# Where the split token rows begin in on-chip memory, and the number of idle matmuls at the start

## The chip, the cores and the metric

The kernel runs as one program on one core of a Trainium2 chip. The metric is the device time of one execution in microseconds, taken as the median of several runs. The engines are TensorE (PE; the profile lists its weight loads apart, as PEld), VectorE (DVE), ScalarE (ACT), GpSimd (POOL) and SyncE (SP), which here only issues DMAs.

## The reference

One layer of a decoder trunk, for 4096 prompt tokens and 64 sample tokens (8 sequences of 8 tokens), width 1024:

```
h = rmsnorm(x) * g_pre
z = h @ w_in                       # 1024 -> 2816 columns, cut into ten groups
A) out_a = silu(cg) * cb * conv3(cc * ch)          # gated short convolution, 256 channels
B) out_b = silu(ag) * window_attention(q, k, v)    # window 128, 8 query heads, 2 kv heads, a sink per head
C) out_c = silu(mg) * memory_attention(mq)         # 4 heads into 256 memory tokens
y = concat(out_a, out_b, out_c) @ w_out            # 1024 -> 1024
x = x + rmsnorm(y) * g_post
```

The outputs are x for all tokens and the new keys, values and convolution rows. Everything is float32.

## The kernel before

**Two stages.** The first stage (`plain_block`, then `input_projection`) computes z for all 4160 tokens and writes the parts of it to DRAM. It takes the first 929 us of the profile. The second stage reads them back in chunks of 256 tokens, does both attentions and the output projection, and takes the rest.

**Split numbers.** TensorE multiplies in the reduced format float32r, so each operand is split in two: `hi` is the value rounded to that format, `lo` is what is left over. A product of two numbers is then three matmuls: hi·w_hi, lo·w_hi, hi·w_lo. `split` and `x_split` make the token halves: ACT writes `hi`, DVE writes `lo = x - hi`. `w_split` makes the weight halves in the same way.

**The first stage's matmuls.** Tokens are cut into 8 blocks of 520, each of two halves of 260 (`HW`). The width 1024 is cut into two halves of four 128-row pieces (`KH = 4`). Blocks 0 and 1 use plain products (8 per block), all others a scheme with 7 products per block (`PRODUCTS`), whose operands are sums and differences of token halves and of weight quarters. The columns of w_in go in three phases of 4, 4 and 3 pairs of 128-column tiles. One call of `product` is 12 matmuls, each with a weight tile of 128x128 (stationary) and 260 tokens (moving), added up in one PSUM bank `c`. There are 768 such matmuls in the plain blocks, 2016 in the rest of phase 0, 2688 in phase 1 and 2016 in phase 2, 7488 in all; every one loads its own weights. DVE adds the banks into the tiles `z` (`evict`).

**Order.** In the plain blocks and phase 0 the order of each engine is the order in which the code is written; later a scheduler sets it, with some instructions pinned.

**Where the operands lie.** An address here is that of a byte in each of the 128 partitions of on-chip memory, as the built program has it. A token half is a tile of four rows of 320 float32 (`XR = 320`), of which the first 260 are used. A row is thus 1280 bytes, 5 times 256, and all four rows of a tile begin at the same address modulo 256. The tiles come from the pool `hp` (two buffers for `hi`, two for `lo`). A weight tile is 2 x 512 float32 from the pools `wa` and `wb`; a matmul reads 128 of them, at a multiple of 512 bytes. The pool `shift` holds one tile of 32 float32 that nothing uses; it stands ahead of `hp` and moves it, and all pools opened after it on that side, by 128 bytes. In the program of before, the token rows and the weights both begin at 224 modulo 256.

Other matmuls of the program with float32r operands, in the same terms (moving operand, then weights, modulo 256):

| matmul | columns | moving | weights | count |
|---|---|---|---|---|
| `c`, first stage | 260 | 224 | 224 | 7488 |
| `y`, output projection (weights `mh`, `ml`) | 512 (256 in the last part) | 224 | 224 | 1560 |
| `y` of the sample tokens (weights `mh_s`) | 512 | 224 | 96 | 32 |
| `ws`, window scores | 256 | 96 or 160 | the same | 512 |
| `xs`, memory scores, odd chunks and the first | 256 | 160 | 160 | 144 |
| `xs`, memory scores, even chunks | 256 | 160 | 96 | 112 |

**The beginning.** While the first tokens and weights are on their way, TensorE runs 14 matmuls on a tile of ones (`idle<-warm`). Their result is not used.

Of the kernel before, what the change touches and what calls it, by code (L numbers as in the profile page):

```python
# [8 lines left out]
F32 = mybir.dt.float32  # L9
F32R = mybir.dt.float32r  # L10
# [5 lines left out]
P = 128  # L16
D = 1024
KT = D // P
KH = KT // 2
# [4 lines left out]
HW = 260  # L24
XR = 320
# [22 lines left out]
def f(ap):  # L48
    return ap.bitcast(F32)
# [3 lines left out]
def hybrid_layer(ctx: ExitStack, tc: tile.TileContext, a: dict):  # L53
# [31 lines left out]
    pa = ExitStack()  # L85
# [3 lines left out]

    place = ctx.enter_context(tc.tile_pool(name="place", bufs=1)).tile([P, 2, KH, HW], F32, name="place")  # L90
    hxp = pa.enter_context(tc.tile_pool(name="hx", bufs=4))
    pa.enter_context(tc.tile_pool(name="shift", bufs=1)).tile([P, 32], F32, name="shift")
    hp = pa.enter_context(tc.tile_pool(name="hp", bufs=2))
    own = ExitStack()
    kept_z = ExitStack()
# [66 lines left out]
    def store(dst, src):  # L162
        if store_queue[0] is G:
            G.dma_start(dst, src)
        else:
            late.append(lambda: DMA.dma_start(dst, src))
# [153 lines left out]
    def gain_of(o, k):  # L320
        kk = KH * (int(o[1]) - 1) + k
        return gpre[:, kk : kk + 1]
# [16 lines left out]
    def t_sum(ph, b, o):  # L339
# [9 lines left out]
        if ph == 1:  # L349
# [2 lines left out]
                tc.keep_in_program_order(ins)  # L352
            store(hd[b][o], ops[o])

    def split(src, name):
        hi = hp.tile([P, KH, XR], F32R, tag="hi", name=f"hi{name}")[:, :, :HW]
        lo = hp.tile([P, KH, XR], F32R, tag="lo", name=f"lo{name}")[:, :, :HW]
        S.copy(hi, src)
        V.tensor_tensor(lo, src, f(hi), op=ALU.subtract)
        return hi, lo  # L360
# [157 lines left out]
    def h_split(i):  # L518
        if i < len(steps):
            ph, b, p = steps[i]  # L520
            o = PRODUCTS[p][1]
            hs[i] = split(xs[ph, b][o], f"{ph}_{b}{o}")
# [52 lines left out]
    raw0, zz, pending, h0, kept = {}, {}, {}, {}, {}  # L575

    def x_split(b, o, meanwhile=lambda: None):
        x = xs[0, b][o]
        h0[b, o] = hi, lo = [hp.tile([P, KH, XR], F32R, tag=n, name=f"{n}0_{b}{o}")[:, :, :HW] for n in ("hi", "lo")]
        for k in range(KH):  # L580
            if k == 1:
                meanwhile()
            g = gain_of(o, k)
            S.mul(hi[:, k], x[:, k], g)
            V.scalar_tensor_tensor(lo[:, k], x[:, k], g, f(hi[:, k]), op0=ALU.mult, op1=ALU.subtract)
# [37 lines left out]
    def plain_jobs(b, s):  # L623

        gains = lambda b, *os: [lambda o=o: x_gain(0, b, o) for o in os]
        scales = lambda b, *os: [lambda o=o: x_scale(0, b, o) for o in os]
        parts = lambda b, o: [lambda: x_split(b, o)]
        fill = lambda o: [lambda q=q: first_fill(o, q) for q in range(4)]
        sums = lambda q, k: [lambda: first_sums(q, k)]
# [70 lines left out]
    idle = accumulator(1, 2, "idle")  # L700
    warm = hp.tile([P, KH, XR], F32R, tag="lo", name="warm").rearrange("p k n -> p (k n)")
    G.memset(f(warm[:, : P + 512]), 1.0)
    for n in (416, 416, 416, 416, 512, 512, 512, 416, 416, 416, 260, 260, 260, 260):
        TE.matmul(idle[:, 0, :n], warm[:, :P], warm[:, P : P + n], start=True, stop=True)  # L704
    x_split(0, "B11", lambda: first_fill("A21", 0))
    for q in range(4):
        if q > 0:
# [743 lines left out]
    class Block:  # L1451
# [10 lines left out]
        def split(self):  # L1462
# [13 lines left out]
            self.hl = [hi, lo]  # L1476

        def run(self, last, start, split, starts):
            b, m = self.b, self.m
            yn = work([P, D], "yn", f"yn{b}")  # L1480
# [4 lines left out]
            for p, (c0, c1) in enumerate(parts):  # L1485
                if p == 1:
                    split()
                acc = psum("z", f"y{b}_{p}")[:, : c1 - c0]
                j, passes = 0, 3 if m == P else 2
                for k in range(KT):  # L1490
                    if k in starts:
                        start()
                    for l, r in ((0, 0), (1, 0), (0, 1)) if m == P else ((0, 0), (0, 1)):
                        TE.matmul(acc, self.hl[l][:, k], wo[k][c0 // 512][:, r, c0 % 512 : c0 % 512 + c1 - c0], start=j == 0, stop=j == passes * KT - 1)  # L1494
                        j += 1
                if m < P:
                    S.copy(yn[:m, c0:c1], acc[m : 2 * m])
                    V.tensor_tensor(acc[:m], acc[:m], yn[:m, c0:c1], op=ALU.add)
                end = last and p == 2
                if not end:  # L1500
                    V.tensor_tensor(yn[:m, c0:c1], acc[:m], gpost[:m, c0:c1], op=ALU.mult)  # L1501
                S.activation((psum("t", "sq") if end else acc)[:m, : c1 - c0], acc[:m], AF.Square, scale=float(D) ** -0.5, accum_out=st[:m, p : p + 1])  # L1502
                if last and p == 1:
                    V.tensor_tensor(st[:m, 0:1], st[:m, 0:1], st[:m, 1:2], op=ALU.add)
# [180 lines left out]
```

## Time and profile before

| | |
|---|---|
| median of 3 runs | 1536.18 us (1535.31 to 1536.74) |
| profiled execution | 1533.46 us, of which the span of the core's instructions is 1531.7 us |
| granted TensorE clock in that execution | 0.999 |
| busy: PE, PEld, DVE, ACT, POOL | 1520.7, 1398.8, 1145.3, 806.1, 380.0 us |

A matmul's duration in the profile (283 ns for one with 260 columns) holds its way through the array, and successive matmuls overlap. What one costs in a long run is therefore read from starts: the start of the last minus the start of the first, over the number between them. The chain of work that ended last names, from the end back, what each step waited for; a piece "PE c L368 x1895" is a run of 1895 matmuls in which none waited for anything but the one before it. The profile prints names without the numbers of buffers, and `c`, `hi`, `lo` and `w` with those of block, quarter and product.

### The profile page before, as it was taken

What the parts mean: (1) busy time and instruction counts of PE and PEld (TensorE: products, weight loads), DVE (VectorE), ACT (ScalarE), POOL (GpSimd) and SP (SyncE); (2) the same over time, 40 slices, a digit from 0 to 9 for tenths busy, and PEclk for the clock granted to TensorE, in tenths of its full rate; (3) what the DMA queues carried; (4) which work ended last, traced back from release to release, by engine and by line L of the source; (5) the groups of instructions that cost most, each with busy time, mean ns of one, the idle gap of its engine ahead of it and who ended that gap; (6) DMA issues with size and microseconds to landing.
All of it is one profiled execution on the core that took longest, in us unless ns stands there. A gap on an engine that the chain in (4) does not pass through costs nothing.

```text
span 1531.7 us, 30162 instructions
## 1 busy us (share of the span) xinstructions
PE 1520.7 (99%) x11337; PEld 1398.8 (91%) x11337; DVE 1145.3 (75%) x2055; ACT 806.1 (53%) x2039; POOL 380.0 (25%) x604
## 2 busy tenths in 40 slices
PE   9999999999999999999999999999999999999998
PEld 9999999999999999999999998788888888888876
DVE  6789888898978777897777679766666666666743
ACT  6786566476222222354454447755665565565632
POOL 0223332221400000000101204544444444444310
PEclk9999999999999999999999999999999999999999
DMA  9989999878755333677877789977777777776332
GB/s 257 199 225 246 274 283 267 277 244 284 194 181 181 127 126 127 225 231 278 229 272 227 230 291 260 239 151 159 148 148 151 155 156 150 160 161 146 131 110 96
DMA packets 177942, 306.28 MB, mean 200 GB/s; under 512 B 33925, under 2 KB 107653, under 8 KB 177765
## 3 DMA queue, kind: packets, MB, share of 16 engines
q1 hardware_dynamic: 130901, 227.38, 48.2%
q0 software_dynamic: 46176, 75.92, 25.1%
q8 instruction: 90, 1.47, 0.4%
q10 hardware_dynamic: 720, 1.05, 0.2%
q14 instruction: 55, 0.45, 0.1%
HBM read 197.23 MB, written 108.05 MB: 199 GB/s over the span
## 4 chain that ended last, share of the span: by engine, by line
PE 93%; DVE 3%; DMA 1%; ACT 1%; issue 1%; POOL 0%; SPq 0%; DVEq 0%; POOLq 0%; ACTq 0%
PE c L368 53%; PE y L1494 23%; PE ws L1248 4%; PE wo L1090 2%; PE wt L1271 2%; PE xs L1184 2%; PE xt L1199 2%; PE wo L1220 2%; PE wo L1226 1%; PE mem_acc L791 1%; DMA nat<-in_x_p 1%; DMA ws18A<-in_w_in 0%; DMA ws20A<-in_w_in 0%; DVE x_2T L348 0%; PE idle L704 0%
## 5 line engine op out<-in xcount | busy, mean ns | idle before, releaser
L1494 PE MATMUL y<-wo,mh 128*128 128x512 f32 (+1 forms) x1040 | 350.1, 399 | 0.0
L375 DVE TENSOR_TENSOR z<-c,z 128x520 f32<-128x520 f32 (+1 forms) x308 | 195.0, 647 | 88.8 <-PE c L368 87.5
L1494 PEld LDWEIGHTS y<-wo,mh 128*128 128x128 f32 x1040 | 194.3, 188 | 39.3 <-issue 2.4
L1494 PE MATMUL y<-wo,ml 128*128 128x512 f32 (+1 forms) x520 | 201.8, 388 | 0.0
L1261 ACT ACTIVATE sm<-sm,wnm 128x128 f32<-128x128 f32 x256 | 99.6, 390 | 61.0 <-DVE wnm L1255 59.7
L1193 POOL TENSOR_SCALAR xp<-xp,xrd 128x256 f32<-128x256 f32 x128 | 74.6, 590 | 207.1 <-DVE xrd L1189 207.0
L1494 PEld LDWEIGHTS y<-wo,ml 128*128 128x128 f32 x520 | 98.2, 189 | 16.2
L1185 DVE TENSOR_REDUCE xmx<-xs 128x2 f32<-128x512 f32 x64 | 44.1, 689 | 59.4 <-PE xs L1184 59.3
L1273 ACT COPY wpt<-wt 128x512 f32<-128x512 f32 x64 | 37.3, 582 | 86.3 <-PE wt L1271 83.7
L1248 PEld LDWEIGHTS ws<-kst,q 128*128 128x128 f32 x512 | 70.0, 190 | 5.4 <-ACT xp L1188 0.7
L1501 DVE TENSOR_TENSOR yn<-y,gpost 128x512 f32<-128x512 f32 (+1 forms) x66 | 45.1, 684 | 39.6 <-PE y L1494 39.3
L1248 PE MATMUL ws<-kst,q 128*128 128x256 f32 x512 | 73.1, 283 | 0.4 <-ACT xp L1188 0.4
L1502 ACT ACTIVATE y<-y 128x512 f32<-128x512 f32 (+1 forms) x66 | 38.6, 585 | 64.2 <-DVE yn L1501 64.2
L739 POOL CAST wmask<-negs 128x256 uint8<-128x256 f32 x1 | 0.6, 610 | 266.4 <-DMA negs<-in_wmask 266.4
L1281 POOL TENSOR_SCALAR_AFFINE_SELECT wpt<-wpt 128x512 f32<-128x512 f32 x64 | 52.8, 824 | 42.1 <-ACT wpt L1273 39.1
L1188 ACT ACTIVATE xp<-xs,xnm 128x256 f32<-128x256 f32 x128 | 58.9, 464 | 7.1 <-DVE xnm L1186 7.1
L1123 POOL DMA_DIRECT2D q<-qd x64 | 42.8, 674 | 71.0 <-DVE wo L186 60.9
L1112 POOL DMA_DIRECT2D kst<-qd x64 | 38.6, 616 | 63.7 <-PE xt L1199 41.5
L1251 DVE COPY_PREDICATED sm<-wmask,ws 128x256 f32<-128x256 uint8 x124 | 52.2, 436 | 2.7 <-ACT sm L1250 2.5
L1512 DVE SCALAR_TENSOR_TENSOR xr<-yn,yst,xr 128x1024 f32<-128x1024 f32 (+2 forms) x34 | 43.1, 1269 | 14.0 <-POOL yst L1508 13.3
L1278 POOL TENSOR_SCALAR_AFFINE_SELECT wpv<-wpt 128x512 f32<-128x512 f32 x62 | 40.2, 648 | 50.9 <-ACT wpt L1273 50.8
L377 ACT COPY z<-c 128x520 f32<-128x520 f32 (+1 forms) x44 | 24.4, 554 | 51.9 <-PE c L368 47.9
(962 smaller groups left out, 5116.4 us busy)
## 6 DMA issues: line engine op xcount, KB each, us to landing
q<-qd POOLq DMA_DIRECT2D x64, 384.0 KB, 8.2
xr<-in_x_p SPq DMA_DIRECT2D x32, 512.0 KB
nat<-in_x_p SPq DMA_DIRECT2D x39, 416.0 KB
o_yp<-xr SPq DMA_DIRECT2D x31, 512.0 KB
md<-th POOLq DMA_DIRECT2D x48, 260.0 KB, 6.5
qd<-zh SPq DMA_DIRECT2D x48, 260.0 KB
qd<-z SPq DMA_DIRECT2D x48, 260.0 KB
kst<-qd POOLq DMA_DIRECT2D x60, 192.0 KB, 5.7
```

The costliest lines, as they stand in the source:

```text
L368: TE.matmul(bank[:, :HW], l, r, start=first and i == 0, stop=last and i == 3 * KH - 1)
L375: add = lambda dst, other: V.tensor_tensor(dst, c, other, op=ALU.add)
L1185: V.tensor_reduce(mx[:, :nb], s, axis=AX.X, op=ALU.max)
L1188: S.activation(p[:, i, :], s[:, i, :], AF.Exp, bias=nm[:, i : i + 1], scale=SCALE, accum_out=den[:, i : i + 1])
L1193: G.tensor_scalar(p[:, i, :], p[:, i, :], rd[:, i : i + 1], 0.5, op0=ALU.mult, op1=ALU.mult)
L1248: TE.matmul(s3[:, hh, :], self.q[:, 4 + 2 * (2 * half + hh) + kvh, i * P : i * P + P], self.kst[:, 2 * kvh + part, i * P : i * P + 2 * P], ...
L1251: V.copy_predicated(sm[:, 2 * half : 2 * half + 2, :], third["wmask"], third["negs"] if first else s3[:, :, 0:P])
L1261: S.activation(sm[:, hh, :], sm[:, hh, :], AF.Exp, bias=nm[:, hh : hh + 1], scale=SCALE, accum_out=den[:, hh : hh + 1])
L1281: G.affine_select(p3, p3, pattern=[[0, 4], [1, P]], compare_op=ALU.is_ge, fill=0.0, base=0, channel_multiplier=-1)
L1494: TE.matmul(acc, self.hl[l][:, k], wo[k][c0 // 512][:, r, c0 % 512 : c0 % 512 + c1 - c0], start=j == 0, stop=j == passes * KT - 1)
L1501: V.tensor_tensor(yn[:m, c0:c1], acc[:m], gpost[:m, c0:c1], op=ALU.mult)
L1512: V.scalar_tensor_tensor(self.xr[:m, cs], yn[:m, cs], st[:m, 3:4], self.xr[:m, cs], op0=ALU.mult, op1=ALU.add)
```

## The change

Three things change in the code:

- the pool `shift` is gone, so `hp` and the pools behind it on that side (`z0` to `z10`, `y0` to `y2`, `nat`, `ones` and the temporary tiles `t0`, `t1`, `t2a`, `t2b`) lie 128 bytes lower; `wa`, `wb`, `place`, `hx` and everything of the second stage lie where they lay;
- a token row begins 16 float32 (64 bytes) into its 320, in `split_tile`, for `hi` and for `lo`. With the 128 bytes less, the rows begin at 160 modulo 256, where they began at 224. The weights stay at 224;
- six of the fourteen idle matmuls are gone.

```diff
-    pa.enter_context(tc.tile_pool(name="shift", bufs=1)).tile([P, 32], F32, name="shift")
...
+    begins = {"hi": 16, "lo": 16}
+
+    def split_tile(tag, name):
+
+        n = begins[tag]
+        return hp.tile([P, KH, XR], F32R, tag=tag, name=name)[:, :, n : n + HW]
+
     def split(src, name):
-        hi = hp.tile([P, KH, XR], F32R, tag="hi", name=f"hi{name}")[:, :, :HW]
-        lo = hp.tile([P, KH, XR], F32R, tag="lo", name=f"lo{name}")[:, :, :HW]
+        hi, lo = split_tile("hi", f"hi{name}"), split_tile("lo", f"lo{name}")
...
-        h0[b, o] = hi, lo = [hp.tile([P, KH, XR], F32R, tag=n, name=f"{n}0_{b}{o}")[:, :, :HW] for n in ("hi", "lo")]
+        h0[b, o] = hi, lo = [split_tile(n, f"{n}0_{b}{o}") for n in ("hi", "lo")]
...
-    for n in (416, 416, 416, 416, 512, 512, 512, 416, 416, 416, 260, 260, 260, 260):
+    for n in (416, 416, 416, 416, 512, 512, 512, 416):
```

No instruction changes its place in the order of any engine. On TensorE, at the beginning of the program, these rows stood before (`idle` is the bank that nobody reads, `w_0A` the first quarter of the weights, `hi_0B` and `lo_0B` the first tokens):

```order
1 L704 MATMUL idle<-warm 128x416 x4
2 L704 MATMUL idle<-warm 128x512 x3
3 L704 MATMUL idle<-warm 128x416 x3
4 L704 MATMUL idle<-warm 128x260 x4
5 L368 MATMUL c_0_0_0_278<-hi_0B_240,w_0A_244 128x260
6 L368 MATMUL c_0_0_0_278<-lo_0B_241,w_0A_244 128x260
7 L368 MATMUL c_0_0_0_278<-hi_0B_240,w_0A_244 128x260 x2
```

And these stand there now:

```order
1 L709 MATMUL idle<-warm 128x416 x4
2 L709 MATMUL idle<-warm 128x512 x3
3 L709 MATMUL idle<-warm 128x416
4 L373 MATMUL c_0_0_0_268<-hi_0B_230,w_0A_234 128x260
5 L373 MATMUL c_0_0_0_268<-lo_0B_231,w_0A_234 128x260
6 L373 MATMUL c_0_0_0_268<-hi_0B_230,w_0A_234 128x260 x2
```

Two idle matmuls of 416 columns and four of 260 are missing; the first product follows the eighth. Lines of the kernel from 352 on have moved by five.

## The prediction

> **What bounds the kernel now.** I read the page first: busy time, the granted clock, the shares of the chain.
>
> ```profile
> span 1531.7 us, 30162 instructions
> ...
> PE 1520.7 (99%) x11337; PEld 1398.8 (91%) x11337; DVE 1145.3 (75%) x2055; ACT 806.1 (53%) x2039; POOL 380.0 (25%) x604
> ...
> PEclk9999999999999999999999999999999999999999
> ...
> PE 93%; DVE 3%; DMA 1%; ACT 1%; issue 1%; POOL 0%; SPq 0%; DVEq 0%; POOLq 0%; ACTq 0%
> PE c L368 53%; PE y L1494 23%; PE ws L1248 4%; PE wo L1090 2%; PE wt L1271 2%; PE xs L1184 2%; PE xt L1199 2%; PE wo L1220 2%; PE wo L1226 1%; PE mem_acc L791 1%; DMA nat<-in_x_p 1%; DMA ws18A<-in_w_in 0%; DMA ws20A<-in_w_in 0%; DVE x_2T L348 0%; PE idle L704 0%
> ```
>
> TensorE is busy nearly all the time at the full granted clock, and 93% of the chain is its work; the last row splits the chain by line. The second view is the chain in order of time, its pieces in the first stage; columns are start, duration, what, and how many.
>
> ```profile
> 6.53 50.52 PE c L368 x420
> ...
> 58.27 24.57 PE c L368 x208
> 82.84 9.36 DMA nat<-in_x_p
> ...
> 112.51 236.80 PE c L368 x1992
> ...
> 428.63 5.35 DMA ws18A<-in_w_in
> ...
> 479.46 225.15 PE c L368 x1895
> ...
> 876.57 52.04 PE c L368 x432
> ```
>
> The 7488 `c` matmuls make 53% of the chain, 0.53 x 1531.7 = 812 us. In the long run of 1895 one costs (225.15 - 0.16) / 1895 = 118.7 ns; 0.16 is the tail of the last one (0.28 long, less one spacing of 0.12). In the last run of 432 the same kind of matmul, with the same addresses modulo 256, costs (52.04 - 0.16) / 432 = 120.1 ns. So the chain holds about 812 / 0.1187 = 6840 of them; the other 650 run while the chain goes through a DMA and what follows it (the rows at 82.84 and 428.63), and their speed counts little as long as it gets no worse.
>
> What do the 118.7 ns consist of? I compare rows of the timeline in the last output blocks, where 512 and 256 columns stand close together (start, duration, line, names, count).
>
> ```profile
> 1506.66 7.61 PE L1494 MATMUL y<-wo,mh_s 128*128 128x512 f32 x32
> 1514.11 0.39 PE L1494 MATMUL y<-wo,mh 128*128 128x512 f32 x1
> ...
> 1517.06 0.39 PE L1494 MATMUL y<-wo,ml 128*128 128x512 f32 x1
> ...
> 1519.10 0.39 PE L1494 MATMUL y<-wo,ml 128*128 128x512 f32 x1
> ...
> 1519.79 0.40 PE L1494 MATMUL y<-wo,mh 128*128 128x256 f32 x2
> ...
> 1521.94 0.28 PE L1494 MATMUL y<-wo,mh 128*128 128x256 f32 x1
> ...
> 1005.41 0.60 PE L1199 MATMUL xt<-ident,xp 128*128 128x128 f32 x4
> ```
>
> Between 1517.06 and 1519.10 lie nine spacings: 226.7 ns for 512 columns. Between 1519.79 and 1521.94 lie eighteen: 119.4 ns for 256. The difference gives 0.419 ns a column, so 260 columns alone would stream in 109 ns. The transposes, four weight loads with 128 columns each, are spaced (0.60 - 0.27) / 3 = 110 ns, which bounds what a weight load alone needs. So a `c` matmul takes some 9 ns more than either of its two reads, and both reads, rows and next weights, run at once. That is the time the change can touch: at most 9 ns of 118.7.
>
> That the place of the reads matters is in the first two rows. The sample tokens' 32 matmuls differ from their neighbours in the weights' begin: 96 modulo 256 against 224 for the moving rows, half of 256 apart. They are spaced (1514.11 - 1506.66) / 32 = 232.8 ns, against 226.7 with equal begins: 6.1 ns more.
>
> **The change, part by part.** *Begin of the rows.* It adds and removes no instruction here; it changes the spacing of 7488 matmuls by an amount for which the trace has no row: moving operand 64 bytes below the weights. I bound it. From above: half of 256 apart costs 6.1 ns, times 7488 = 46 us, less the 2 us that TensorE waits in the first stage anyway:
>
> ```profile
> PE c L368 <- DVE lo_2T L359: 1.4, 2, 0.9
> PE c L368 <- DVE lo_3T L359: 0.3, 1, 0.3
> PE c L368 <- DVE lo_0T L359: 0.2, 1, 0.2
> ```
>
> that is +44. From below: the weight load's own 110 ns, 8.7 less than now; only the 6840 on the chain gain, -60 us. The nearest row is a quarter apart with the other sign, the memory scores of an even chunk (moving 160, weights 96), beside an odd chunk (both 160):
>
> ```profile
> 1026.90 0.64 PE L1184 MATMUL xs<-mk,q 128*128 128x256 f32 x4
> ...
> 1063.63 0.63 PE L1184 MATMUL xs<-mk,q 128*128 128x256 f32 x4
> ```
>
> Four matmuls in 0.64 against 0.63 us: a quarter apart is not like half apart, and costs nothing that these rows can tell. So the place is near no change, and the sign open. I take a gain of 2.0 ns, a third of the 6.1 ns by which the only visible change of place moves a spacing. The sign is a choice, for this reason: with equal begins the same matmul settles at 118.7 in one run and 120.1 in another, both far over the 109 and 110 of its parts, so equal begins are a place where the two reads get into each other's way, and where it depends on the entry how much. A quarter off, they may settle lower. 2.0 x 6840 = -13.7 us.
>
> The Trainium skill speaks against any effect: TensorE: Matmul & The Clock Gate, in the step-by-step of part 2, says that TensorE has two independent read ports, and that loading the next weights takes no bandwidth from the running matmul. The trace disagrees for these operands: 118.7 ns stand against 109 and 110, and 232.8 against 226.7. By the page's spacing for N columns, N / 2.4 + 2.5, a `c` matmul would take an estimated 111 ns and the place would be free; taken as a rival this is "no change" below.
>
> *Writers of the rows.* ACT and DVE now write to the new place; reads of x come from four buffers that begin at four different places modulo 256 (32, 96, 160, 224), and the split takes the same time for all blocks:
>
> ```profile
> L359 DVE TENSOR_TENSOR lo_2T<-x_2T,hi_2T x8: 1231/1243/1244, 111.2 to 754.4; 128x1040 fp32r<-128x1040 f32 x8
> L359 DVE TENSOR_TENSOR lo_3T<-x_3T,hi_3T x8: 1228/1243/1245, 148.8 to 788.3; 128x1040 fp32r<-128x1040 f32 x8
> ```
>
> so I cost the new place of these tiles, and the 128 bytes by which `z` and the temporaries move, at nothing. What hides a small difference is DVE's slack: it is busy 75% of the span. Were that cover gone, 1% on DVE's chain pieces, 3% of the span, would be 0.5 us.
>
> *Idle matmuls.* Rows of the start:
>
> ```profile
> 2.16 4.37 PE L704 MATMUL idle<-warm 128*128 128x416 f32 x14 [2.16 <-POOL warm L702]
> ...
> 6.36 0.28 PE L368 MATMUL c<-hi_0B,w_0A 128*128 128x260 f32 x1
> ...
> 5.09 0.60 ACT L182 CAST w_0A<-wr_0A 128x512 fp32r<-128x512 f32 x1
> ...
> 10.04 0.62 ACT L182 CAST w_3A<-wr_3A 128x512 fp32r<-128x512 f32 x1 [1.01 <-DMA wr_3A<-in_w_in]
> ...
> 10.70 0.69 DVE L186 TENSOR_TENSOR w_3A<-wr_3A,w_3A 128x512 fp32r<-128x512 f32 x1 [0.93 <-ACT w_3A L182]
> ...
> 11.44 0.51 PE L368 MATMUL c<-hi_0B,w_3A 128*128 128x260 f32 x2
> ```
>
> The fourteen have 5488 columns, the eight 3616; at the same rate they end 4.37 x 1872 / 5488 = 1.5 us sooner, and the first `c` can start when ACT has w_0A, 5.69, not 6.36. That 0.67 us buys nothing: the third matmul of w_3A needs DVE's half at 11.39, which hangs on the DMA of wr_3A, and it starts at 11.44 either way. Only with those weights earlier would the 0.67 count. A risk stands on the other side: the fourteen are far slower than streaming (4.37 us against 5488 x 0.419 = 2.3), so the clock is low at first, which the row of 38-us slices can't show, and a pause may keep it low. The 38 matmuls ahead of 11.44 need 4.5 us at full speed and have 5.75, so 1.2 us are free; were all 38 at half speed, 3.3 us would be lost. I take 0, ends -0.7 and +3.3.
>
> *Sum.* -13.7 + 0 + 0 on the profiled 1533.46 us (span 1531.7, 1.8 around it) is 1519.8; the median lies 2.7 higher, so I predict 1536.18 - 13.7 = 1522.5.
>
> **Rivals.** *No change:* the pair settles at the same 118.7; the near-equal `xs` rows speak for it. 1536.
>
> *It settles at 120.1 throughout,* as in the run of 432. What for: 256 columns settle at 119.4 too, so this looks like a common resting place; against: the 118.7 of nearly all runs. 1.4 x (7488 - 432, which are there already) = +9.9, 1546.
>
> *It behaves as half apart,* +44, 1580. For: the `mh_s` row; against: the `xs` rows. This decides as soon as the spacing passes 119.1 (0.4 ns x 7488 = 3 us); it and the last rival are one mechanism, the two reads meeting more often.
>
> *Transfers bind first.* If TensorE is quicker, loads must keep up:
>
> ```profile
> 150.00:200.00 50.00, 50.00 (x424) 50.00 (x423) 40.75 (x50) 29.95 (x51) 14.29 (x23) 1.00 1.02 298
> ...
> 500.00:550.00 50.00, 50.00 (x424) 50.00 (x423) 39.98 (x57) 15.41 (x19) 0.00 (x0) 1.00 0.38 128
> ```
>
> The share of the DMA engines, next to last, is full between 150 and 250 and slack in phase 1. At 2% that stretch may give back 2 us of the gain: 1524, inside the first case.
>
> **How the numbers follow.** Quicker rows 0.46 (own range 1498 to 1533: from 5.5 ns to 0.5 ns a matmul); no change 0.17; 120.1 0.19; half apart 0.13; 0.05 for what I don't see, on the slow side. A measurement of this kernel can't tell 0.2%, 3.1 us, from nothing. Faster 0.46, within 0.18 (no change and a little of its neighbours), slower 0.36. The range takes the first three cases, nearly all of each, and what lies between 1546 and 1565 of the half-apart case: 1500 to 1565.
>
> **What would show it.** The chain's long runs of `c` tell each case: a run of 1895 should last 221.3 us at 116.7 ns; 225 is no change, 227.7 the 120.1, 236.7 half apart. `y`, `ws` and `xs` must keep their spacings, since none of their operands moves; if they change, my reading by address is wrong. The third matmul of w_3A should still start near 11.4; later than 12 means that the clock stayed low. I am wrong above all if the sign of a quarter below differs from what I chose, and partly if phase 0 shows new waits of `c` for DMA.

## The result, and the profile after

The changed kernel took 1542.33 us (median of 17 runs, 1540.98 to 1544.53), the kernel before, on the same chip, 1536.12 (17 runs, 1532.60 to 1542.92). The ratio is 1.0045, 95% interval 1.0036 to 1.0053: slower by 0.45%, where 1522.5 and a gain had been forecast. The profiled execution took 1542.29 us.

The page of the changed kernel, the same rows as before:

```profile
span 1540.6 us, 30150 instructions
...
PE 1529.7 (99%) x11331; PEld 1408.0 (91%) x11331; DVE 1146.2 (74%) x2055; ACT 806.0 (52%) x2039; POOL 379.4 (25%) x604
...
PEclk9999999999999999999999999999999999999999
...
PE 94%; DVE 2%; DMA 2%; issue 1%; ACT 1%; POOL 0%; DVEq 0%; POOLq 0%; ACTq 0%; SPq 0%
```

TensorE is busy 9.0 us longer at the same granted clock, and its weight loads, which run with it, 9.2 us; the other engines hardly changed. The chain of waits in the first stage (start, duration, what, count) says where:

```profile
6.40 52.59 PE c L373 x420
...
114.24 239.32 PE c L373 x1992
...
356.70 354.49 PE c L373 x2950
...
884.71 34.77 PE c L373 x288
```

The run of 1992 lasts 239.32 us and lasted 236.80. The run of 1895 and those ahead of it in phase 1 are now one of 2950: the short waits between them are gone. The starts of the matmuls in the trace, fitted with a line, give the spacing to a hundredth: 120.00 ns in every long run after; before, 118.67 ns in all long runs but the last, of 432, which had 120.00. That is the quantity of this case, and below "spacing" always means this fit. (A piece of the chain, less the tail of 0.16 us and divided by its count as in the prediction, gives 0.06 to 0.13 more, as a piece begins a little ahead of its first matmul.)

The waits of TensorE, largest first (us in total, times, longest), behind the 2.2 us that the idle matmuls wait for `warm` in both kernels:

```profile
PE c L373 <- ACT w_0A L181: 0.9, 1, 0.9
PE wt L1276 <- DVE xrd L1194: 0.7, 1, 0.7
PE ws L1253 <- ACT xp L1193: 0.4, 1, 0.4
PE c L373 <- DVE lo_0T L364: 0.2, 1, 0.2
```

The 1.7 us for lo_2T and lo_3T are gone, since a slower TensorE comes later to its operands. New are 0.9 us at the beginning, ahead of the first product, and 0.7 us of a wait in the second stage, which varies: it was 1.7 us in a second profile of the kernel before (experiment 11). The beginning, from the timeline of TensorE:

```profile
2.16 3.38 PE L709 MATMUL idle<-warm 128*128 128x416 f32 x8 [2.16 <-POOL warm L707]
6.40 0.58 PE L373 MATMUL c<-hi_0B,w_0A 128*128 128x260 f32 x1 [0.86 <-ACT w_0A L181]
6.78 0.42 PE L373 MATMUL c<-lo_0B,w_0A 128*128 128x260 f32 x1
7.12 0.80 PE L373 MATMUL c<-hi_0B,w_0A 128*128 128x260 f32 x2
...
12.98 0.40 PE L373 MATMUL c<-hi_0B,w_3A 128*128 128x260 f32 x2
...
1515.53 7.61 PE L1499 MATMUL y<-wo,mh_s 128*128 128x512 f32 x32
1522.97 0.39 PE L1499 MATMUL y<-wo,mh 128*128 128x512 f32 x1
```

After a pause of 0.86 us the first three products are 345 to 383 ns apart and the next ones 215 to 219 ns, until some 10.2 us. The third matmul of w_3A starts at 12.98, where it started at 11.44. The last two rows are the sample tokens' 32 output matmuls, whose operands did not move: (1522.97 - 1515.53) / 32 = 232.5 ns, as before.

*Account of the 8.9 us of span.* The run of 432 had the 120.00 already, so 6840 - 432 = 6408 matmuls of the chain are 1.33 ns dearer: +8.5. Plain block 1 starts 1.9 later, 0.5 of it is the spacing again (384 x 1.33), so the slow beginning is +1.4. Waits on lo_2T and lo_3T: -1.7; the wait in the second stage: +0.7. Sum 8.9. The starts of all `c` matmuls give the same by another way: 9.3 for the spacing of some 7000 of them, +1.4 in plain block 0, and -2.5 for the pauses between runs elsewhere, the waits just named among them. That makes 8.2 for the first stage, whose last `c` starts at 936.47 and started at 928.33.

### The profile page after: what moved, and what is told of

It reads as the page before. It is cut to its first block, busy times and chain, and to the rows that moved or that the text cites. A ratio compares the mean times of both kernels' runs of the same rounds, so it can differ in the third digit from the quotient of the medians.

```text
span 1540.6 us, 30150 instructions
## 1 busy us (share of the span) xinstructions
PE 1529.7 (99%) x11331; PEld 1408.0 (91%) x11331; DVE 1146.2 (74%) x2055; ACT 806.0 (52%) x2039; POOL 379.4 (25%) x604
## 4 chain that ended last, share of the span: by engine, by line
PE 94%; DVE 2%; DMA 2%; issue 1%; ACT 1%; POOL 0%; DVEq 0%; POOLq 0%; ACTq 0%; SPq 0%
PE c L373 55%; PE y L1499 22%; PE ws L1253 4%; PE wo L1095 2%; PE wt L1276 2%; PE xs L1189 2%; PE xt L1204 2%; PE wo L1225 2%; PE wo L1231 1%; PE mem_acc L796 1%; DMA qd<-z 1%; DMA nat<-in_x_p 1%; DMA xr<-in_x_p 0%; DVE wo L185 0%; DMA wr_0A<-in_w_in 0%
```

## The experiments

Two theories. **Distance:** the distance of the rows' begin from the weights', modulo 256, decides at which spacing the stream of `c` matmuls settles. **Entry:** the way in which the stream starts (here: the idle matmuls) decides it, and the place is free. A third, for the rows' own place, stands in experiment 3. All kernels but 1, 11 and 12 keep the new `split_tile` without the pool `shift` (experiment 3 has other pools instead) and have fourteen idle matmuls where nothing else is said. The rows quoted are pieces of the chain of waits of the kernel named.

**1. Eight idle matmuls alone**, rows at 224.

```diff
-    for n in (416, 416, 416, 416, 512, 512, 512, 416, 416, 416, 260, 260, 260, 260):
+    for n in (416, 416, 416, 416, 512, 512, 512, 416):
```

> Only the idle matmuls of the change (eight in place of fourteen); the rows stay at 224, like the weights. If the begin of the rows sets the spacing of the c matmuls: 118.7 ns in the long runs as before (run of 1895: 225 us), and the only loss is at the start, where TensorE is slower in the first 20 us: plain block 0 longer by about 1.3 us, the whole 1.0 to 2.0 us (0.1%) above the kernel before. Rival, the way in which the stream is entered picks the spacing: 120.0 ns from the first product on, 225 becomes 227.4, the whole some 6 us above before. Rival, the idle matmuls are free: no difference, and the first product starts about 0.7 us sooner.

1535.58 us against 1533.39, ratio 1.0012 (1.0002 to 1.0021).

```profile
112.07 236.79 PE c L368 x1992
...
478.42 227.67 PE c L368 x1895
```

The run of 1992 keeps 118.67, so the entry does not set the spacing throughout. But the run of 1895 has 120.00, 2.5 us more than before: with equal begins there are two resting places. Plain block 0 is not longer: plain block 1 starts at 52.80, against 52.61 before. The 1.0 to 2.0 us were met in the time by the ratio (1.8 us, 0.3 to 3.2), though the medians lie 2.2 apart, and not in their place: the profile's own excess is the run of 1895.

**2. The rows alone**, at 160, fourteen idle matmuls.

> Only the begin of the rows (160, weights at 224); all fourteen idle matmuls. If the begin sets the spacing: 120.0 ns throughout as in the changed kernel, and the time 4.5 to 5.5 us above before (the changed kernel's 6.2 less the 1.3 of the start). If the entry through the idle matmuls sets it: 118.7 ns, and no difference from before.

1542.28 us against 1533.39, ratio 1.0060 (1.0046 to 1.0074): 9.2 us, 7.1 to 11.3. The kind was right, the size was not: I had derived 4.5 to 5.5 from the first comparison, in which the kernel before had the higher median (1536.12).

```profile
113.11 239.32 PE c L373 x1992
...
483.95 227.68 PE c L373 x1895
```

All long runs are at 120.00. The rows alone bring the loss.

**3. Rows and weights both at 160.**

```diff
+    ctx.enter_context(tc.tile_pool(name="aside", bufs=1)).tile([P, 48], F32, name="aside")
     wa = ctx.enter_context(tc.tile_pool(name="wa", bufs=3 * NP_))
...
+    wb_stack.enter_context(tc.tile_pool(name="bside", bufs=1, side="right")).tile([P, 16], F32, name="bside")
...
+    begins = {"hi": 32, "lo": 32}
```

> Rows and first-stage weights both begin at 160, fourteen idle matmuls; everything else on that side of the memory moves along. If what counts is the distance between rows and weights (0 as before): 118.7 ns in the long runs, phases as long as before. If what counts is the place 160 of the rows: 120.0 ns. The second stage should not care.

```profile
483.63 225.15 PE c L375 x1895
```

The spacing is 118.67 ns in all long runs, and the piece lasts what it lasted before, to the hundredth. So at 160 it is the distance between the two reads that counts, not the place of the rows. In one point the expectation failed: phase 1 begins at 345.19, against 340.33 before, since the long run of phase 0 begins 5 us later, after waits of TensorE for `mix_s` and `lo_2B` (1.7 and 1.6 us) that the kernel before does not have. Phases 1 and 2 are shorter than before (320.70 and 266.01 us against 321.39 and 266.61). One execution was taken, of 1538.56 us.

**4 to 8. The distance, and a control.** One number changes, `begins`: 0, 48, 24, 40 and, for the control, 32 float32.

| experiment | `begins` | rows at | distance to the weights |
|---|---|---|---|
| 4 | 0 | 96 | 128 |
| 5 | 48 | 32 | 64 above |
| 6 | 24 | 192 | 32 below |
| 7 | 40 | 0 | 32 above |
| 8 | 32 | 224 | 0 |

> Rows at 96, weights at 224, half of 256 apart; fourteen idle matmuls. By the spacing that the sample tokens' y matmuls show at half apart (6.1 ns more for 512 columns): 120 to 125 ns a matmul, the first stage 9 to 46 us longer than before. If the spacing at 160 was a matter of any distance but zero: 120.0 ns again, +9 us at most in the first stage. If the distance does not matter: 118.7 ns.

> Rows at 32, weights at 224: a quarter of 256 apart as in the changed kernel, but 64 bytes above the weights and not below; fourteen idle matmuls. If only the amount counts: 120.0 ns in the long runs. If the sign counts, as the prediction's working had it with the wrong sign: 116.7 ns or at least under 118.7. If any distance but zero costs the same as half apart: 120.0 to 121.1.

> Rows at 192, 32 bytes below the weights; fourteen idle matmuls. If the spacing grows with the distance (118.7 at 0, 120.0 at 64, 120.0 to 121.1 at 128): between 118.7 and 120.0. If there is a step at the first distance that is not zero: 120.0.

> Rows at 0, 32 bytes above the weights; fourteen idle matmuls. If only the amount counts: the same as at 192 (32 below). If the sign counts: different from it, and on the other side of 118.7.

> Control: the pool that shifts is gone and the rows begin 128 bytes into their 1280, so that they begin at 224 like the weights, as before; z and the temporary tiles lie 128 bytes lower, as in the changed kernel; fourteen idle matmuls. If the begin alone counts: 118.7 ns in most runs (120.0 in single runs, as before), first stage as long as before within 2.5 us. If the lower place of z and the temporaries counts: 120.0 ns.

The run of 1895, in the order 4 to 8:

```profile
485.28 229.77 PE c L373 x1895
```

```profile
483.94 227.67 PE c L373 x1895
```

```profile
484.57 227.67 PE c L373 x1895
```

```profile
483.93 227.67 PE c L373 x1895
```

```profile
478.85 225.14 PE c L373 x1895
```

Half apart, the spacing is 121.11 ns in a little over half of the matmuls and 120.00 in the others (1547.60 us, one execution as for all of these). At 64 above, 32 below and 32 above it is 120.00 everywhere (1543.80, 1542.55, 1541.98 us). At 32 and 64 there is neither a sign nor a slope. The control has 118.67, and 120.00 in the last run of 432, as before (1534.87 us), so the lower place of z and the temporaries is free. Control and experiment 2 are the cleanest pair, since both start `c` at 6.90: their last `c` matmuls start at 927.68 and 936.87, 9.19 us apart, where 1.33 x 7056 would be 9.4. Rows of one window of both, first experiment 2, then the control (window, length, TensorE busy with `c` and count, weight loads, clock, DMA share, GB/s):

```profile
100.00:340.00 240.00, 239.90 (x1999) 239.69 (x1998) 1.00 0.92 258
```

```profile
100.00:340.00 240.00, 239.74 (x2020) 239.53 (x2019) 1.00 0.92 259
```

In the same 240 busy microseconds 21 fewer `c` matmuls begin; the busy time shows nothing, the count does.

**9. Only the lo rows at 160.**

```diff
-    begins = {"hi": 16, "lo": 16}
+    begins = {"hi": 32, "lo": 16}
```

> Only the lo halves begin at 160; the hi halves and the weights at 224; fourteen idle matmuls. A third of the c matmuls streams lo rows. If each matmul has a price by its own distance: 118.7 + a third of 1.33 = 119.1 ns on average, first stage some 3 us longer than before. If the spacing is a state that the whole stream falls into: 120.0 ns for all, first stage some 8 us longer, as with both halves moved.

```profile
113.30 239.45 PE c L373 x1992
...
484.48 227.66 PE c L373 x1895
```

The spacing is 120.00 in nearly all runs, with 118.86 to 118.95 in a few short ones (one of 215), and not 119.1 on average (1543.29 us, one execution): moving the third of the matmuls that streams lo rows costs as much as moving all (the last `c` starts at 936.96, in experiment 2 at 936.87). In these runs the stream settled as a whole.

**10. Rows at 208**, 16 bytes below (`begins` 28).

> Rows at 208, 16 bytes below the weights; fourteen idle matmuls. If any distance breaks the 118.7: 120.0 ns, first stage some 8 us longer than before. If memory is read in pieces of 32 bytes and only the piece counts, 208 lies in another piece than 224 (192 to 223): 120.0 as well; if 64-byte pieces count (192 to 255): 118.7 here, but then 192 should have had it too. So 118.7 here would mean that only distances of 32 and more count.

```profile
113.00 236.82 PE c L373 x1992
...
479.69 225.14 PE c L373 x1895
```

The spacing is 118.67, with some short runs at 120.00; 1533.78 us. 16 bytes below cost nothing, and the theory of 32-byte pieces falls.

**11 and 12. The kernel before, and the one with eight idle matmuls, once more.**

> The kernel before once more, for a second profile. If the spacing of a long run is fixed by the program: 118.7 ns everywhere and 120.0 in the last run of 432, as in the first profile. If it is drawn anew in each execution: other runs at 120.0.

> Eight idle matmuls and rows at 224 once more, for a second profile of the start and of the long runs. If eight idle matmuls put the run of 1895 at 120.0 by way of the entry: 227.4 us again. If that was drawn: 225 in this one. The start: the clock doubles somewhere between the first product and 10 us in both profiles, and plain block 1 begins between 52.6 and 54.0 us.

The runs of 1895, first 11, then 12:

```profile
479.06 227.67 PE c L368 x1895
```

```profile
478.80 225.14 PE c L368 x1895
```

They have changed sides: the kernel before has 120.00 here (1537.26 us), the one with eight 118.67 (1533.84 us). So with equal begins the program does not fix the resting place; it differs from one execution to another, as if drawn, and experiment 1's long run was such a draw. A part of the chip in this is not excluded, since the two profiles of the kernel with eight come from two chips. Against it speaks that 11 and 12 ran on the same chip and differ, and that the 17 executions of the kernel before on one chip reach from 1532.60 to 1542.92 us. In 12 the third matmul of w_3A starts at 11.15, earlier than before.

**13 to 15. Within 32 bytes:** 16 above (`begins` 36), 24 below (26), 4 above (33).

> Rows at 240, 16 bytes above the weights; fourteen idle matmuls. If the band in which the 118.7 is to be had is symmetric: 118.7, as at 16 below, first stage about as long as before. If it ends at the weights' own begin on this side (a sign after all): 120.0 ns, first stage some 9 us longer. A spacing under 118.7 would be the gain that the prediction had looked for.

> Rows at 200, 24 bytes below the weights; fourteen idle matmuls. If the band reaches to any distance under 32 bytes: 118.7. If only distances up to 16 keep it: 120.0. If the spacing slides with the distance: between the two.

> Rows at 228, 4 bytes (one number) above the weights; fourteen idle matmuls. If there is a band: 118.7. If a begin that is not a multiple of 16 or 32 has a price of its own: above 120.0. Under 118.7 would be a gain.

Pieces of 13, 14 and 15:

```profile
479.86 224.51 PE c L373 x1895
...
876.34 51.37 PE c L373 x432
```

```profile
488.05 227.66 PE c L373 x1895
...
766.34 13.20 PE c L373 x108
```

```profile
87.55 275.78 PE c L373 x2221
...
497.12 227.68 PE c L373 x1895
```

At 16 above the spacing is 118.33, under that of before, and 118.38 in the last run of 432; 1532.37 us. At 24 below it is 120.00 and in short runs 122.22 (1549.40 us). One float32 above, it is 124.17 up to some 366 us and in the last run of 432, and 120.00 or 123.33 between (1560.42 us, the slowest of all). So there is no band of small distances that is free: 4 bytes cost the most, 18.3 us of the first stage over experiment 2. The time at 24 below must not be laid to the spacing. The span is 7.4 us over that of experiment 2, but the 122.22 makes only 1.5 of it; 3.5 lie in plain block 1 (a wait of 1.7 us and a low clock behind it, see below) and 1.8 in the second stage. Nor do 13 to 15 tell distance from place: the weights stayed at 224 in all experiments but 3, so a begin at 200 or 228 may be dear by itself.

**16 to 18. Rows at 240 timed, with fourteen idle matmuls (16) and with eight (17, the changed kernel with one number different), and rows at 16**, 48 above (18, `begins` 44).

```diff
-    begins = {"hi": 16, "lo": 16}
+    begins = {"hi": 36, "lo": 36}
```

> The kernel with rows at 240 and fourteen idle matmuls again, now timed. Its first profile had 118.33 ns a matmul against 118.67 and 120.0. If that holds in most executions: 0.33 x 6840 = 2.3 us and up to 0.7 us more from the last run of 432, so 2 to 4 us below the kernel before, 0.15% to 0.25%. If it was drawn once: no difference.

> The changed kernel with one number different: rows begin 36 and not 16 float32 into their 320, at 240; eight idle matmuls. If the begin carries the loss: 2 to 4 us below the kernel before as in the run with fourteen, 9 us below the changed kernel. If eight idle matmuls cost something of their own (1.2 us by the first comparison, 0.3 to 3.2): 1 us above the run with fourteen.

> Rows at 16, 48 bytes above the weights; fourteen idle matmuls. If what helps at 240 is an odd multiple of 16: 118.3 here too. If it is a distance under 32: 120.0 ns or more.

Against 1533.86 us before, 16 took 1534.01, ratio 0.9999 (0.9990 to 1.0008), and 17 took 1535.26, ratio 1.0008 (0.9995 to 1.0020). Pieces of 16, 17 and 18:

```profile
112.38 236.25 PE c L373 x1992
...
478.81 227.67 PE c L373 x1895
```

```profile
485.40 224.51 PE c L373 x1895
```

```profile
112.11 217.31 PE c L373 x1823
...
479.96 225.86 PE c L373 x1895
```

The 118.33 is there in most runs, but it is drawn like the 118.67: in 16 the run of 1895 fell to 120.00, which takes back 3.2 us. In the time nothing is left of the gain, and no version here beats the kernel before measurably. But one number takes the changed kernel's loss away. (The profiled execution of 17 is the slowest of its twelve, 1541.34 us, in spite of its 118.33: waits and a low clock ahead of the run of 1992, see below, let it begin at 119.16, where it begins at 112.38 in 16.) At 48 above all long runs have 119.05 (1535.75 us, one execution), so an odd multiple of 16 is not the rule for 118.3 either.

*The beginning with eight and with fourteen.* In the sixteen profiles with fourteen idle matmuls the third matmul of w_3A starts between 11.37 and 12.27. In the four with eight it starts at 11.15, 11.74, 12.89 and 12.98 (experiments 12, 1, 17 and the changed kernel). Experiment 17, and then 12, from the timeline:

```profile
8.67 0.42 PE L373 MATMUL c<-hi_0B,w_0A 128*128 128x260 f32 x1
...
12.89 0.40 PE L373 MATMUL c<-hi_0B,w_3A 128*128 128x260 f32 x2
```

```profile
10.91 0.28 PE L368 MATMUL c<-hi_0B,w_3A 128*128 128x260 f32 x1
...
11.15 0.40 PE L368 MATMUL c<-hi_0B,w_3A 128*128 128x260 f32 x2
```

How long TensorE runs at half its pace is on record. The trace keeps a list of stretches with the clock that was granted in each. Its first stretch, at 1.00, begins where the spacing of the idle matmuls or the products falls to about half: between 5.32 and 8.36 us in the sixteen profiles with fourteen, at 5.17 and 5.42 in experiments 12 and 1, and at 10.93 and 10.35 in experiment 17 and the changed kernel. So with eight the full clock came either while the idle matmuls still ran, or 2 us later than it ever did with fourteen. Experiment 12 had expected the clock to double after the first product; it had doubled at 5.17, ahead of the first product at 5.66.

A low clock came back once in experiment 17 and once in 14, after TensorE had waited 2.4 and 1.7 us ahead of `rows_y` in plain block 1. The record has 0.50 there, from 62.13 to 65.54 and from 61.48 to 64.89 us, and the products are 215 to 219 ns apart again. Experiment 17, the wait (us in total, times, longest) and a window inside the stretch (window, length, then busy time and count of TensorE, weight loads, VectorE, ScalarE and GpSimd, clock, DMA share, GB/s):

```profile
PE rows_y L303 <- DVE mix_s L294: 2.4, 1, 2.4
```

```profile
62.20:65.20 3.00, 3.00 (x16) 3.00 (x15) 1.70 (x4) 3.00 (x7) 0.00 (x0) 0.50 0.89 220
```

The Trainium skill, TensorE: Matmul & The Clock Gate, section "What's actually happening", has a free-running window of 3.4 us at whose end the clock is set by how busy TensorE was, so that the number of slow matmuls varies between runs. The trace agrees: both stretches at 0.50 last 3.41 us, and the sixteen times at which the full clock came with fourteen lie within 3.04 us. That the pause behind the eight idle matmuls left such a window too idle in two of four executions fits the dates, but was not tried.

## Why the prediction was wrong, point by point

*What bounds the kernel* was right: TensorE's 7488 `c` matmuls, and nothing but their spacing. That the two reads, rows and next weights, set it through their relative begin is what experiments 2, 3 and 8 show: 120.00, 118.67 and 118.67 ns.

*The step that failed is the sign in "Begin of the rows"*: -2.0 ns a matmul taken, +1.33 measured. The argument was that equal begins are where the reads get into each other's way, since 118.7 and 120.1 both lie far over 109 and 110, and that a quarter off they may settle lower. The runs show the reverse: the term of -13.7 us measures +8.5 by the same reckoning. 120.00 is the place into which the stream falls at 32 and 64 bytes; lower ones were met in long runs only with equal begins, 16 bytes off, or 48 above (119.05). A place under 118.67 exists, 16 bytes above the weights, and gives 0.33 ns, not 2.0. The row that the prediction held for an oddity, the 120.1 in the run of 432, was the common case.

*A row was too coarse.* The `xs` rows, 0.64 against 0.63 us for four matmuls, were read as "a quarter apart costs nothing". Over three spacings a step of 0.01 us is 3.3 ns, and the effect is 1.33. The starts in that same trace are finer: from 985 us on, the 28 groups of four in odd chunks have 117.2 ns, the 24 in even chunks 118.6. So a quarter apart (there the rows lie 64 bytes above) was 1.4 ns dearer, the size and the sign of what came, and it could be read before any run. The same fault lies in the choice of 2.0 ns as a third of 6.1: the 6.1 belong to 512 columns, and at half apart the `c` matmuls were 2.4 ns dearer at most.

*The rival that came true* is "settles at 120.1 throughout", which had 0.19 and gave +9.9 us; measured +6.2. That 1542.33 lies inside the stated 1500 to 1565 is due to it and not to the sum. Its spacing term was 1.4 us too large (8.5: 1.33 and not 1.4 ns, and the matmuls beside the chain do not count). The beginning and the waits add 1.4 - 1.7 + 0.7 = 0.4, which makes the 8.9 between the two profiles. The last 2.7 lie between the profiled execution of before, 1533.46, and its median in this comparison, 1536.12: its executions differ, in part by their draws: experiment 11 has one of 1537.26 with the run of 1895 at 120.00, 2.5 us more than at 118.67.

*Idle matmuls:* 0 taken, ends -0.7 and +3.3. The profiles show a loss of 1.2 to 1.4 us in two of four executions and none in two; the timed pairs give 2.2 us (experiment 1; by the ratio 1.8, 0.3 to 3.2) and 1.3 us (17 against 16, whose intervals overlap). The term is between 0 and some 2 us, and these runs do not say closer. The risk that the prediction named, a clock that stays low, is what the record shows: the full clock comes at 10.35 us in the changed kernel and came at 5.70 before. The marker was too tight: 12.98 did mean a slow beginning, but six profiles with fourteen pass 12 too (12.07 to 12.27). A view can mislead here, since it prints 1.00 where the trace has no record, as ahead of the 10.35 (columns as above):

```profile
6.00:10.00 4.00, 3.60 (x15) 3.38 (x16) 3.29 (x7) 3.52 (x8) 0.00 (x0) 1.00 1.00 323
```

Fifteen matmuls in 3.60 busy microseconds are 240 ns each.

*Writers of the rows* were rightly costed at nothing: lo_2T takes 1238 ns (median), where it took 1243. `y`, `ws` and `xs`, whose operands had not moved, kept their spacings (on average 229.8 ns for 512 columns, 119.0, and by chunk 117.2 or 118.6). *Transfers bind first* did not arise.

*Independent ports.* The prediction weighed the Trainium skill, TensorE: Matmul & The Clock Gate, section "Step-by-step: what each phase is for", by which two independent read ports let the next weights load at no cost to the running matmul. This is not borne out for these operands: the same matmul takes 118.3 to 124.2 ns as the begin of its rows moves. The prediction also drew 111 ns and "no change" from the page's N / 2.4 + 2.5. But the Trainium skill, TensorE: Matmul & The Clock Gate, section "Back-to-back issue gap", gives that spacing for isolated matmuls and says that in a stream of weight loads and matmuls both set it. The trace agrees with the latter, with 118.7 ns over the 109 and 110 of the parts, so the 111 ns were no forecast for this stream.

## What to carry to other kernels

When two operands of a stream are read at once, their begins modulo 256 are a parameter with a price, here 1% of the first stage (9.2 of 928 us) between equal begins and 64 bytes. Test it with both operands moved together and with one alone. The two distances that were no multiple of 16 bytes, 4 and 24, had the highest spacings of all (124.17 and 122.22 ns). Read a spacing from hundreds of starts, not from a group of four, when the effect is a nanosecond. A kernel whose executions fall into two resting places can have a wide spread in its times (1532.6 to 1542.9 before, 1541.0 to 1544.5 after), and one profile shows one draw of it. Before a difference of a few microseconds between two single profiles is laid to the change, look for it by stage: waits and a low clock made 3.5 us of the difference between experiments 14 and 2 and 6.5 us of that between 17 and 16.

## What had not been expected of the hardware

- The spacing of a 260-column `c` matmul, by the distance of rows from weights (the weights at 224): 118.67 or 120.00 ns at 0 and 16 below; 118.33 or 120.00 at 16 above; 119.05 at 48 above; 120.00 at 32 on both sides and 64 on both sides; 120.00 or 121.11 at 128; 120.00 or 122.22 at 24 below; 120.00, 123.33 or 124.17 at 4 above. Why these values, no run tells.
- A stream keeps its spacing for up to 2000 matmuls on end, and where several spacings are possible, executions of the same kernel differ (225.15 and 227.67 us for the same 1895 matmuls).
- Behind a wait of TensorE of 1.7 or 2.4 us in plain block 1 the granted clock fell to 0.50 for 3.41 us, with matmuls 215 to 219 ns apart (experiments 14 and 17). Behind waits of 1.7 and 1.8 us in the second stage of the same executions it stayed at 1.00.
